# Attention's TensorE order rewritten, with two PSUM banks for the outputs and two for the projections

## The chip, the cores and the metric

The kernel runs on one core of a Trainium2 chip. The time is the device time of one execution in microseconds; the median over several executions is compared. In the profile, PE is TensorE's matmuls, PEld its weight loads, DVE VectorE, ACT ScalarE, POOL GpSimd and SP the engine that issues most transfers.

## The reference

One layer of a hybrid encoder over 1024 positions of width 1024, in float32. The part that matters here is the token mixer:

```python
h = modulate(rms_norm(x, g_pre_mix), sh1, sc1)
bg, cg, u, q, k, v, ga, gb = split(h @ w_in)
y_conv = (bg * causal_dwconv3(cg * u)) @ w_proj_conv
# stick-breaking attention, 8 heads of 64, strictly causal
a[t, s] = sigmoid(z_ts) * prod_{s < j < t} (1 - sigmoid(z_tj)),  z = q k^T / 8
y_attn = (a @ v) @ w_proj_attn
out = (sigmoid(ga) * y_conv + sigmoid(gb) * y_attn) @ w_out
```

A squared-ReLU MLP of width 4096 follows, with a norm and a gate of its own.

## The kernel before

A float32 value is held as a sum of two parts of the type float32r, a high and a low one, and a product is three matmuls (high by high, high by low, low by high). Splitting a tile is a copy on ACT (L104, the high part) and a subtraction on DVE (L91, the low part).

The stage in question runs from about 86 to 437 us. It computes attention for 8 heads and, between attention's steps, the projections of h onto queries, keys and the three inputs of the convolution. Attention is cut into 32 units, one for each head and each group g (0 to 3) of 256 query rows; unit number = 4 x head + g. PE's instructions in this stage stand in an order written out by hand, the string `order`: one word (window) for each unit, one letter for each step.

- `f` is one step of `fill`: one eighth of the contraction of half a projection, three matmuls of 128x512 (`project`, L547). Eight such steps fill one bank; 20 projections of two halves give 320 steps, of which 289 stand in the order and 31 run after it. After the eighth, `use` reads the bank: ACT and DVE copy queries (L569, L570) or keys (L588, L589, L590), DVE or ACT the convolution's inputs (L600, L609, L628).
- `n` is one step of `weights` for the next unit: two matmuls into a bank `z` (L678, L681) for up to 512 keys. ACT then forms two sigmoids (L684 into `pt`, L685 into `a`); when a block of 128 rows is complete, POOL masks its diagonal (L687), DVE runs the product scan over the row (L691) and multiplies (L695). The result is `a`.
- `w` is one step of `attend`: in turns a `turn` (three or four 128x128 transposes of `a` into a bank `tr`, L721, which are then split into `tu` by L104 and L91) and a `weigh` (four matmuls of `tu` with the values into the bank `o`, L732). A weigh stands one turn behind its own transposes, so the last weigh of a unit is the second `w` of the next unit's window. After it `finish` reads the bank with ACT (L741) and DVE (L742, `ot`), and stores. The next unit's first weigh is two `w` steps further on.

The other engines' orders in this stage are made by the framework's scheduler from this program; only PE's is by hand. Of the eight PSUM banks `psm` (tag `mm`) has three, and the pool `pat` has `z` two, `tr` two, `o` one. With one `o` bank a unit's first weigh waits for L742 of the unit before. Writing T(u,k) and W(u,k) for the turn and the weigh number k of unit u, the text below can name steps: unit 9's window `nnffwnffnwffwfwf` holds T(9,0), the last weigh of unit 8, T(9,1) and W(9,0).

After the order is used up, `conv_branch` runs the remaining `fill` steps, with DVE and ACT in an order of the program's.

Of the kernel before, what the change touches and what calls it, by code (L numbers as in the profile page):

```python
# [13 lines left out]
PSUM = bass.MemoryType.PSUM  # L14
# [16 lines left out]
def block_kernel(  # L31
# [28 lines left out]
    def nm(s):  # L60
        uid[0] += 1
        return f"{s}_{uid[0]}"

    def open_pool(es, name, **kw):
        kw = {"bufs": 1, "reuse_waits": "tile", **kw}
        return es.enter_context(tc.tile_pool(name=name, **kw))
# [14 lines left out]
    def bank(pool, tag, bufs=None):  # L81
        return pool.tile([P, HALF], F32, tag=tag, name=nm(tag), bufs=bufs)
# [19 lines left out]
    def split(src, hi, lo, eng=nc.vector):  # L102

        nc.scalar.copy(hi, src)  # L104
        sub(lo, src, f(hi), eng)

    def load_cols(w, m):

        raw = raw_tile((P, KC, P))
        nc.sync.dma_start(raw, w[:, m * P : (m + 1) * P].rearrange("(a p) n -> p a n", p=P))  # L110
        hi = wp.tile([P, KC, P], F32R, tag="wh", name=nm("wh"), bufs=2)
        lo = wp.tile([P, KC, P], F32R, tag="wl", name=nm("wl"), bufs=2)
        split(raw, hi, lo)
        return hi, lo
# [421 lines left out]
        with tc.manual_schedule(engines={mybir.EngineType.PE, mybir.EngineType.SP}):  # L536
            run(order)
    psm_es = ExitStack()
    psm = open_pool(psm_es, "psm", bufs=3, space=PSUM, side="right")


    def project(ps, w, half):

        s = halves[half]
        for k in range(KC):
            for i, (a, b) in enumerate(((0, 0), (0, 1), (1, 0))):
                nc.tensor.matmul(  # L547
                    ps, w[a][:, k, :], hT[b][:, k, s], start=k == 0 and i == 0,
                    stop=k == KC - 1 and i == 2, skip_group_check=True,
                )  # L550
            yield k

    with ExitStack() as es:
        at = open_pool(es, "at")
        pat = open_pool(es, "pat", space=PSUM)
# [78 lines left out]
        def projections(seq):  # L634
            ahead = load_cols(w_in, seq[0][1])
            for n, (begin, m, j) in enumerate(seq):
                w = ahead
                if n + 1 < len(seq):
                    ahead = load_cols(w_in, seq[n + 1][1])
                use = begin(j)  # L640
                for half in range(2):
                    ps = bank(psm, "mm")
                    for k in project(ps, w, half):
                        if k == KC - 1:
                            use(half, ps)
                        yield
# [9 lines left out]
        for p, (n0, n1) in enumerate(CONV):  # L656
            seq += rest[:n0] + qk[2 * p + 2 : 2 * p + 4] + rest[n0 : n0 + n1]
            rest = rest[n0 + n1 :]
        fill = projections(seq + rest)

        def weights_of(hd, i, out):
# [42 lines left out]
        def attend(hd, g, aa):  # L704

            p, e = hd // 2, hd % 2
            own, other = slice(e * HD, (e + 1) * HD), slice((1 - e) * HD, (2 - e) * HD)
            parts, po = {}, None

            def turn(jp):  # L710
                diag = jp == g
                pa = bank(pat, "tr", 2)
                th, tl = parts[jp] = turned[seen[0] % 2]
                seen[0] += 1
                pa3 = pa.rearrange("p (a b) -> p a b", b=P)
                for j in range(2):
                    for t in range(2):
                        if diag and j > t:
                            continue
                        s = (2 * jp + j) * P  # L720
                        nc.tensor.transpose(pa3[:, 2 * j + t, :], aa[t][:, s : s + P], ident)  # L721
                for b in ((slice(0, 2), slice(3, 4)) if diag else (slice(0, 4),)):
                    to = slice(b.start + 1, b.stop + 1)
                    split(pa3[:, b, :], th[:, to, :], tl[:, to, :])

            def weigh(jp):
                nonlocal po
                po = po if jp else bank(pat, "o", 1)
                for j in range(2):
                    v = vs[:, 2 * jp + j, hd, :, :]  # L730
                    for n, part in enumerate(parts[jp]):
                        nc.tensor.matmul(  # L732
                            po[:, : 2 * P], v,
                            part[:, 0:5:4, :] if j and jp == g else part[:, 2 * j + 1 : 2 * j + 3, :],
                            start=jp == 0 and j == 0 and n == 0,
                            stop=jp == g and j == 1 and n == 1,
                        )

            def finish():
                ot = at.tile([P, 2 * P], F32, tag="ot", name=nm("ot"), bufs=1)  # L740
                nc.scalar.copy(ot[own], po[other, : 2 * P])  # L741
                nc.vector.tensor_tensor(ot[own], po[own, : 2 * P], ot[own], op=ALU.add)  # L742
                nc.sync.dma_start(o_d[p, own, 2 * g * P : (2 * g + 2) * P], ot[own])


            for jp in range(g + 1):
                turn(jp)
                yield
                if due:
                    due.pop()()  # L750
                    yield
                due.append(lambda jp=jp: (weigh(jp), jp == g and finish()))
# [5 lines left out]
        for t in turned:  # L758
# [4 lines left out]


        order = """
            ffffffffffffffffffffffffffffffffnffffffnfffffff
            nnfwf ffnnfwfnffwwnfwf nfnwwwnfffwwwnf fnfffffwfffwfwfwnwwffwfffw
            nfwnw fffnwwnfffnfnwffffw nfnwwnnffwffwww nwwwfwwwwnw
            nnfwwf nnffwnffnwffwfwf nfwwnffwnwnfwwf fffwfwfffwwnfwnwwfwff
            wnwn fnffffffwfwfwfnfnnffffw fwwnnwfffnnwwffw ffnfnfffffwfwfwffwfwffwfwfffw  # L770
            wnnwf ffnfnfwwwnffnwf nfffwfwnnwwfwnfwf nfffwffnfwffwfwwfwfwfw
            fwnwfn fffnffwnfnnwwffffffw wfnfwffnwwnwnfffwfffff nnffwfwfwfwffwfffwwfffw
            wnwn fffnnfwwnffnww fnffwwwnffnfnfwww fnffwfwwfnfwwfwfwwff
            wfffnnwffff fnfnwfnwfwfnfwf nfffwwnwnfwfnfwffwf fffffwwfwffwwffffwfwfffwf
        """
        with tc.manual_schedule(engines={mybir.EngineType.PE}):
            for u, window in enumerate(order.split(), -1):
# [766 lines left out]
```

## Time and profile before

| | |
|---|---|
| median of 3 runs | 1422.18 us (1419.94 to 1425.4) |
| profiled execution, its own time | 1429.52 us |
| its span in the profile | 1427.8 us |
| mean granted TensorE clock | 0.989 |
| PE / PEld / DVE / ACT / POOL busy | 96% / 79% / 74% / 46% / 7% |

The profiled execution's time is its span and 1.7 us around it; it was 7.3 us above the median. A matmul's end in the profile is modelled: a 128x512 matmul is shown with 0.39 us, and the next starts 0.23 us after it. So a row of PE that waited shows a wait counted from the modelled end.

### The profile page before, as it was taken

How to read it: one execution, taken by the hardware profiler on the slowest of the kernel's cores; microseconds unless marked ns; L12 is line 12 of the kernel's file. 1: busy time of each engine (PE TensorE's matmuls, PEld its weight loads, DVE VectorE, ACT ScalarE, POOL GpSimd, SP SyncE). 2: the span in 40 equal slices, each digit the busy share in tenths (PEclk: the TensorE clock that was granted, in tenths of full speed). 3: DMA queues.
4: the chain of work that ended last, by engine and by line, in shares of the span. 5: the costliest groups of instructions: out<-in, count | busy, mean ns of one | idle time of the engine just before them, and what ended most of it. 6: DMA issues, size and time to landing. Idle time of an engine off the chain costs nothing.

```text
span 1427.8 us, 17929 instructions
## 1 busy us (share of the span) xinstructions
PE 1370.1 (96%) x6281; PEld 1121.9 (79%) x6281; DVE 1059.4 (74%) x1664; ACT 652.4 (46%) x1317; POOL 93.8 (7%) x188
## 2 busy tenths in 40 slices
PE   5899899999999999999999899999999999999997
PEld 4788777887888888777878688888888888888886
DVE  6727887887876877727736886666554989898988
ACT  5636656665543544334446643333331554334343
POOL 1002111211200000000001000000000000000001
PEclk9899999999999999999999899999999999999999
DMA  8601111111123766728432254243336643414113
GB/s 298 189 15 34 38 30 45 38 37 51 37 95 111 257 232 226 236 103 325 147 105 91 72 170 140 90 140 132 125 117 230 199 141 110 158 46 155 56 59 118
DMA packets 112753, 178.42 MB, mean 125 GB/s; under 512 B 7900, under 2 KB 67344, under 8 KB 112664
## 3 DMA queue, kind: packets, MB, share of 16 engines
q1 hardware_dynamic: 112664, 177.29, 37.3%
q8 instruction: 49, 0.80, 0.2%
q14 instruction: 40, 0.33, 0.1%
HBM read 135.83 MB, written 41.43 MB: 124 GB/s over the span
## 4 chain that ended last, share of the span: by engine, by line
PE 74%; DVE 13%; issue 4%; DMA 4%; ACT 3%; POOL 1%; SPq 0%; DVEq 0%; POOLq 0%; ACTq 0%
PE s L235 27%; PE s L1397 18%; PE mm L547 10%; PE s L904 3%; PE v L509 3%; DVE pt L691 2%; PE s L122 2%; PE s L121 2%; PE s L123 2%; PE o L732 2%; DVE a L695 2%; PE tr L721 2%; DMA wa<-in_w_ada_dram 1%; DVE y L91 1%; DMA raw<-in_w_in_dram 1%
## 5 line engine op out<-in xcount | busy, mean ns | idle before, releaser
L1397 PE MATMUL s<-y,y 128*128 128x512 f32 x1008 | 238.5, 390 | 0.0
L1397 PEld LDWEIGHTS s<-y,y 128*128 128x128 f32 x1008 | 189.2, 188 | 40.4
L547 PE MATMUL mm<-hTh,wh 128*128 128x512 f32 x320 | 129.1, 403 | 0.0
L547 PE MATMUL mm<-hTh,wl 128*128 128x512 f32 x320 | 125.5, 392 | 0.0
L547 PE MATMUL mm<-hTl,wh 128*128 128x512 f32 x320 | 125.5, 392 | 0.0
L104 ACT CAST y<-g 128x512 fp32r<-128x512 f32 x96 | 53.1, 619 | 116.7 <-PE s L1397 97.6
L691 DVE TENSOR_TENSOR_SCAN pt<-pt,dmask 128x128 f32<-128x128 f32 (+3 forms) x64 | 87.2, 1366 | 8.6 <-ACT pt L684 8.2
L235 PE MATMUL s<-mTh,g 128*128 128x512 f32 x256 | 87.1, 405 | 3.7 <-ACT mTh L104 3.7
L1397 PE MATMUL s<-fr,fr 128*128 128x512 f32 x336 | 85.9, 392 | 0.2
L104 ACT CAST tu<-tr 128x512 fp32r<-128x512 f32 (+2 forms) x112 | 49.1, 439 | 78.2 <-PE tr L721 49.4
L91 DVE TENSOR_TENSOR tu<-tr,tu 128x512 fp32r<-128x512 f32 (+2 forms) x112 | 55.1, 493 | 34.5 <-ACT tu L104 33.4
L235 PE MATMUL s<-mTh,h 128*128 128x512 f32 x240 | 79.6, 398 | 0.0
L1397 PEld LDWEIGHTS s<-fr,fr 128*128 128x128 f32 x336 | 62.9, 188 | 15.1 <-DVE fr L91 1.1
L1407 DVE TENSOR_TENSOR ffacc<-s,ffacc 128x512 f32<-128x512 f32 x96 | 65.0, 684 | 12.1 <-PE s L1397 12.0
L132 POOL TENSOR_TENSOR rstd<-var,mhalf 128x1 f32<-128x1 f32 x32 | 22.4, 698 | 766.6 <-DVE var L129 766.5
L235 PE MATMUL s<-y,g 128*128 128x512 f32 x288 | 71.7, 391 | 0.0
L235 PE MATMUL s<-y,h 128*128 128x512 f32 x288 | 71.2, 391 | 0.0
L547 PEld LDWEIGHTS mm<-hTh,wl 128*128 128x128 f32 x320 | 60.2, 188 | 13.4
L547 PEld LDWEIGHTS mm<-hTl,wh 128*128 128x128 f32 x320 | 60.5, 189 | 8.9
L547 PEld LDWEIGHTS mm<-hTh,wh 128*128 128x128 f32 x320 | 60.4, 189 | 8.8
L235 PE MATMUL s<-hTh,t 128*128 128x512 f32 x208 | 66.8, 392 | 0.0
L732 PE MATMUL o<-tu,vs 128*128 128x256 f32 x320 | 56.9, 297 | 9.6 <-DVE ot L742 5.0
(292 smaller groups left out, 3124.6 us busy)
## 6 DMA issues: line engine op xcount, KB each, us to landing
raw<-in_w_in_dram SPq DMA_DIRECT2D x38, 512.0 KB, 4.1
raw<-in_w_mlp_in_dram SPq DMA_DIRECT2D x32, 512.0 KB, 3.9
wa<-in_w_ada_dram SPq DMA_DIRECT2D x24, 512.0 KB, 4.4
f_d<-wl SPq DMA_DIRECT2D x16, 512.0 KB, 5.0
f_d<-wh SPq DMA_DIRECT2D x16, 512.0 KB, 4.8
g<-in_w_mlp_out_dram SPq DMA_DIRECT2D x32, 256.0 KB, 3.5
g<-f_d SPq DMA_DIRECT2D x32, 256.0 KB, 4.0
h<-in_w_mlp_out_dram SPq DMA_DIRECT2D x32, 256.0 KB, 3.3
```

Of the source, the lines that this page charges most:

```text
L91: eng.tensor_tensor(o, a, b, op=ALU.subtract)
L104: nc.scalar.copy(hi, src)
L121: nc.tensor.matmul(ps, lh, rh, start=i == 0, stop=False)
L122: nc.tensor.matmul(ps, lh, rl, start=False, stop=False)
L235: nc.tensor.matmul(ps, l, r, start=first and k == 0 and j == 0, stop=k == nk - 1 and j == 2, skip_group_check=True,)
L509: nc.tensor.matmul(vb[b], l, r, start=k == 0 and i == 0, stop=k == KC - 1 and i == 2, skip_group_check=True,)
L547: nc.tensor.matmul(ps, w[a][:, k, :], hT[b][:, k, s], start=k == 0 and i == 0, stop=k == KC - 1 and i == 2, skip_group_check=True,)
L691: nc.vector.tensor_tensor_scan(pt[:, 0:w][:, ::-1], pt[:, 0:w][:, ::-1], dmask[:, T - w : T][:, ::-1], 1.0, ALU.mult, ALU.max,)
L732: nc.tensor.matmul(po[:, : 2 * P], v, part[:, 0:5:4, :] if j and jp == g else part[:, 2 * j + 1 : 2 * j + 3, :], start=jp == 0 and j == 0 ...
L904: nc.tensor.matmul(ps, l[:, k, s], r, start=k == 0 and i == 0, stop=k == 3 and i == 2, skip_group_check=True,)
L1397: nc.tensor.matmul(ps, l[:, s], r, start=start and j == 0 and n == 0, stop=stop and j == len(fs) - 1 and n == 2, skip_group_check=True,)
L1407: nc.vector.tensor_tensor(o, ps, o, op=ALU.add)
```

## The change

Three edits in one:

- `o` gets two banks in turn in place of one.
- `psm` has two banks in place of three. The first projection (queries of the first two heads) uses the two `o` banks, which are not needed until the second window.
- The order is written anew. Each window holds the same `n` and `w` steps as before, and the total of `f` steps is the same (289); their places, and the number of `f` steps in most windows, differ by one to three.

```diff
-    psm = open_pool(psm_es, "psm", bufs=3, space=PSUM, side="right")
+    psm = open_pool(psm_es, "psm", bufs=2, space=PSUM, side="right")
...
-                    ps = bank(psm, "mm")
+                    ps = bank(pat, "o", 2) if n == 0 else bank(psm, "mm")
...
-                po = po if jp else bank(pat, "o", 1)
+                po = po if jp else bank(pat, "o", 2)
...
-            ffffffffffffffffffffffffffffffffnffffffnfffffff
-            nnfwf ffnnfwfnffwwnfwf nfnwwwnfffwwwnf fnfffffwfffwfwfwnwwffwfffw
-            nfwnw fffnwwnfffnfnwffffw nfnwwnnffwffwww nwwwfwwwwnw
-            nnfwwf nnffwnffnwffwfwf nfwwnffwnwnfwwf fffwfwfffwwnfwnwwfwff
-            wnwn fnffffffwfwfwfnfnnffffw fwwnnwfffnnwwffw ffnfnfffffwfwfwffwfwffwfwfffw
-            wnnwf ffnfnfwwwnffnwf nfffwfwnnwwfwnfwf nfffwffnfwffwfwwfwfwfw
-            fwnwfn fffnffwnfnnwwffffffw wfnfwffnwwnwnfffwfffff nnffwfwfwfwffwfffwwfffw
-            wnwn fffnnfwwnffnww fnffwwwnffnfnfwww fnffwfwwfnfwwfwfwwff
-            wfffnnwffff fnfnwfnwfwfnfwf nfffwwnwnfwfnfwffwf fffffwwfwffwwffffwfwfffwf
+            ffffffffffffffffffffffffffffffffnffffffnfffffff nnfffw fnnfwfnfffwwnwf fnfnfwwfwnfwwfnfw
+            ffnfffffwffwffwfwnwwfwffw wnfnw ffnfwnwfffnfnwfffw nfnwwnnffwfffwww
+            nwwwwwwnww nwnwff nnffwnwfnffffwfw nffwnfwnfwwfnwwf
+            ffffwfwfwwnfwnwwwfff wnwn fnffffffwfwnfffnwnfffw ffffwwfnnwffnnwwffw
+            fnfnfffffwfwfwffwfwfwfwffffw nwnfw ffnfnwwwnffnfw nfffwwnnfwwffwnfwf
+            nfffffwfnfwwfwffwffwwfw nwnw fffnffwnfffwnnwffffffw fwnwnfwwnwnfffwffff
+            nnffwfwfwfwfffwfffwwffw wnfnw ffnnfwwnffnwfw fnffwwwnffnfwnfwfwf
+            fnffwfwwfnwwfwffwfw wnfnfwfffff fnfnwffnnwffwwf nfffwwnnwwffnfwffwf
+            fffffwfwwffwwfffwfwfffwf
```

The first window (47 letters) belongs to unit 0's `n` steps and is unchanged; the windows of units 0 to 31 follow.

## The prediction

> **What bounds the kernel now.** I read the page's head first, then the windows by stage, then PE's timeline through attention for the rows that waited.
>
> ```profile
> span 1427.8 us, 17929 instructions
> PE 1370.1 (96%) x6281; PEld 1121.9 (79%) x6281; DVE 1059.4 (74%) x1664; ACT 652.4 (46%) x1317; POOL 93.8 (7%) x188
> ```
> ```profile
> core 0: us, PE busy (x) PEld busy (x) DVE busy (x) ACT busy (x) POOL busy (x), PEclk, DMA share, GB/s
> 120.00:418.00 298.00, 282.44 (x1527) 236.89 (x1526) 241.96 (x337) 173.85 (x388) 60.91 (x129) 0.99 0.14 40
> 418.00:437.00 19.00, 19.00 (x85) 15.70 (x84) 15.68 (x22) 4.27 (x6) 0.00 (x0) 1.00 0.41 135
> ```
>
> PE is the bound nearly everywhere. In the 298 us in which the order is at work it is idle for 15.6 us by the modelled ends; DVE is busy for 242 of them, 81%, so there is room on DVE on average, though not everywhere. Every instruction that PE issues here stays, so the time can only come out of PE's waits (or go into new ones). These are all the rows of PE that waited, 19 of them:
>
> ```profile
> 134.86 0.74 PE L732 MATMUL o<-tu,vs 128*128 128x256 f32 x4 [0.22 <-DVE ot L742]
> 136.46 0.62 PE L732 MATMUL o<-tu,vs 128*128 128x256 f32 x3 [0.41 <-DVE tu L91]
> 168.95 0.55 PE L721 MATMUL tr<-ident,a 128*128 128x128 f32 x3 [0.42 <-DVE a L695]
> 174.69 0.73 PE L732 MATMUL o<-tu,vs 128*128 128x256 f32 x4 [0.42 <-DVE ot L742]
> 178.74 1.01 PE L732 MATMUL o<-tu,vs 128*128 128x256 f32 x3 [2.87 <-DVE tu L91]
> 186.90 0.62 PE L732 MATMUL o<-tu,vs 128*128 128x256 f32 x3 [0.25 <-DVE tu L91]
> 193.51 0.55 PE L721 MATMUL tr<-ident,a 128*128 128x128 f32 x3 [0.78 <-DVE a L695]
> 200.60 0.74 PE L732 MATMUL o<-tu,vs 128*128 128x256 f32 x4 [1.56 <-DVE ot L742]
> 209.15 0.62 PE L732 MATMUL o<-tu,vs 128*128 128x256 f32 x3 [0.34 <-DVE tu L91]
> 212.98 0.52 PE L721 MATMUL tr<-ident,a 128*128 128x128 f32 x3 [0.35 <-DVE a L695]
> 240.43 0.55 PE L721 MATMUL tr<-ident,a 128*128 128x128 f32 x3 [2.02 <-DVE a L695]
> 275.19 0.74 PE L732 MATMUL o<-tu,vs 128*128 128x256 f32 x4 [0.15 <-DVE ot L742]
> 285.99 0.62 PE L732 MATMUL o<-tu,vs 128*128 128x256 f32 x3 [0.71 <-DVE tu L91]
> 315.16 0.55 PE L721 MATMUL tr<-ident,a 128*128 128x128 f32 x3 [0.47 <-DVE a L695]
> 335.08 0.74 PE L732 MATMUL o<-tu,vs 128*128 128x256 f32 x4 [1.88 <-DVE ot L742]
> 348.75 0.55 PE L721 MATMUL tr<-ident,a 128*128 128x128 f32 x3 [0.50 <-DVE a L695]
> 355.55 0.55 PE L721 MATMUL tr<-ident,a 128*128 128x128 f32 x3 [0.26 <-DVE a L695]
> 365.35 0.55 PE L721 MATMUL tr<-ident,a 128*128 128x128 f32 x3 [0.66 <-DVE a L695]
> 388.10 0.74 PE L732 MATMUL o<-tu,vs 128*128 128x256 f32 x4 [0.80 <-DVE ot L742]
> ```
>
> They sum to 15.1 us in three kinds: six weighs that wait for the one `o` bank (L742, 5.0), five that wait for their own split (L91, 4.6), eight turns that wait for `a` (L695, 5.5). The price of a step, and what a row understates, from a quiet stretch:
>
> ```profile
> 398.77 0.64 PE L732 MATMUL o<-tu,vs 128*128 128x256 f32 x4
> 399.25 0.40 PE L547 MATMUL mm<-hTh,wh 128*128 128x512 f32 x1
> 399.48 0.40 PE L547 MATMUL mm<-hTl,wh 128*128 128x512 f32 x1
> 399.94 0.40 PE L547 MATMUL mm<-hTh,wh 128*128 128x512 f32 x1
> ```
>
> A weigh costs 0.48 (398.77 to 399.25), an `f` step 0.69 (399.25 to 399.94). One matmul follows the other after 0.23 but is shown 0.40 long, so each wait costs 0.17 more than its bracket: 15.1 + 19 x 0.17 = 18.3 us. That is the most that this change can take out as waits.
>
> **The change part by part.** *The second output bank* removes the wait for L742 at all six: 5.0 + 6 x 0.17 = 6.0 us. What is late next at each? Two places matter:
>
> ```profile
> 175.67 2.28 DVE L691 TENSOR_TENSOR_SCAN pt<-pt,dmask 128x1024 f32<-128x1024 f32 x1
> 177.99 0.69 DVE L91 TENSOR_TENSOR tu<-tr,tu 128x512 fp32r<-128x512 f32 x1
> ```
> ```profile
> 332.80 0.40 PE L547 MATMUL mm<-hTh,wl 128*128 128x512 f32 x1
> 333.28 0.69 DVE L91 TENSOR_TENSOR tu<-tr,tu 128x512 fp32r<-128x512 f32 x1
> ```
>
> At 174.69 PE would come 0.59 earlier (0.42 + 0.17), but three microseconds on it stands until DVE has run a 2.28 scan and the L91 behind it (177.99); DVE sets that time, so the 0.59 comes back in the next wait. At 335.08 PE could start at 332.80 + 0.23 = 333.03, but its own split ends at 333.28 + 0.69 = 333.97: 0.94 of the 2.05 stays. For the other four I hand back 0.3 (134.86, where the new word has one `f` less between T(2,0) and W(2,0)). Net 6.0 - 0.6 - 0.9 - 0.3 = 4.2 us.
>
> *The turns that wait for `a`.* I count the PE work between a unit's last `n` and its first turn in the old and the new words. It moves by: unit 6 (row 168.95) one `f` less; 9 (193.51) a short turn less, 0.25; 11 (212.98) the same; 14 (240.43) two `f` more; 22 (315.16) 0.2 more; 25 (348.75) 0.2 less; 26 (355.55) one `f` more; 27 (365.35) an `f` and a little more, 0.9. With the time at which `a` is ready left as it is, the eight losses (bracket + 0.17) go from 0.6, 0.95, 0.5, 2.2, 0.65, 0.65, 0.45, 0.8 to 1.3, 1.2, 0.5, 0.8, 0.45, 0.85, 0, 0: 6.8 to 5.1, a gain of 1.7.
>
> *The weighs that wait for their split.* Unit 18 (285.99) has one `f` more between T(18,1) and its weigh, a gain of 0.7; 2 and 10 (136.46, 209.15) cancel at 0.45 each; unit 6 (178.74) has one `f` more, but comes earlier by the 0.59 above and stays; 186.90 stays. Gain 0.7.
>
> *New places.* Units 7 and 8, 16, 17 and 29 lose cover without waiting now: window 7 has no `f` left between its turns (`nwwwwwwnww`), T(17,0) has an `f` less ahead of it, W(16,0) one and a half, W(29,1) two and a bit, less what PE gains at 388. Their slack stands in no row quoted here; each is bounded by nothing and by about an `f`, so 0 to 2.8 together. The rows that wait by a turn's cover (0.4 to 0.9) are nearest, so I charge 0.5 for each of the four, 2.0.
>
> *Two projection banks.* A half may start only when the half two before it is evacuated, in place of three before. The tightest places:
>
> ```profile
> 113.54 0.69 DVE L590 TENSOR_TENSOR kl<-mm,ks 64x512 fp32r<-64x512 f32 x1 [0.49 <-ACT ks L589]
> 330.95 0.69 DVE L590 TENSOR_TENSOR kl<-mm,ks 64x512 fp32r<-64x512 f32 x1 [1.24 <-ACT ks L589]
> ```
> ```profile
> 114.28 0.39 PE L547 MATMUL mm<-hTh,wh 128*128 128x512 f32 x1
> 331.20 0.40 PE L547 MATMUL mm<-hTh,wh 128*128 128x512 f32 x1
> ```
>
> The first pair touches (evacuated at 114.23, next use of that bank under two at 114.28), the second overlaps by 0.44; the new words put half an `f` more into the second. The other halves stand farther apart. I charge 0.4; the ends are 0 and, if the other engines' order slips by half an `f` at each of the sixteen halves of queries and keys, 16 x 0.35 = 5.6. The first projection in the two `o` banks meets no weigh: unit 0's first weigh comes in window 1. Whether those banks come free later than the ones used now is open; all banks of the stage before are read by
>
> ```profile
> 85.34 2.73 DVE L91 TENSOR_TENSOR vs<-v,vs 128x512 fp32r<-128x512 f32 x4 [7.68 <-ACT vs L104]
> ```
>
> 88.07, and PE starts here at 86.6, so 0 to 1.5; I take nothing, since no start of the present banks is late. DMAs: the order moves weight loads by a window at most, in a stage where the engines are busy at a 0.14 share; nothing.
>
> Sum: 4.2 + 1.7 + 0.7 - 2.0 - 0.4 = 4.2 us less. The profiled span goes from 1427.8 to 1423.6, and its time from 1429.5 to 1425.3; in the median's terms, 1422.2 x (1 - 4.2/1427.8) = 1418.0, 0.3% faster. A measurement of this kernel tells about 0.5%, 7.1 us, from no change.
>
> **The clock.** One wait has a consequence of its own:
>
> ```profile
> 178.00:185.00 7.00, 6.26 (x25) 5.74 (x26) 4.87 (x9) 2.14 (x6) 0.50 (x3) 0.52 0.04 9
> ...
> 330.00:340.00 10.00, 8.12 (x46) 6.65 (x45) 5.37 (x10) 3.91 (x10) 1.25 (x4) 1.00 0.27 85
> ```
>
> After the 2.87 us at 178.74 the granted clock is 0.52 for 7 us; around the 1.88 us at 335.08 it is 1.00. At half clock PE does 3.4 us less work there. Little of it is to be won: in that stretch turns and weighs stand back to back, and at full clock each would wait for its split instead. I take 0 in the sum, with 3.4 as the far end. The Trainium skill (TensorE: Matmul & The Clock Gate, HAM oscillation) puts the limit at idle gaps above about 3.4 us; by that a gap of 2.87 would have cost no clock and nothing could be won by shortening it. The trace disagrees with it here, by its 0.52.
>
> **The rivals.** *The waits only move to DVE.* For it: where PE waits longest DVE is full (the scan and L91 above stand back to back), and PE that comes earlier meets the same DVE queue. Against it: 81% busy over the stage, and one of the three largest waits (335.08) stood beside 5.4 of 10 us of DVE (the 330 row above). It gives the gain of that row alone, 1.1, less the bank's 0.4: 1421.5.
>
> *Two projection banks stop PE.* The slower one: ACT and DVE take evacuations in the scheduler's order, among splits and scans; with a bank less, a late L590 or L570 stops not only the projection but, since PE runs in order, every step behind it, and DVE's next scan with it. For it: the two pairs above, without margin. It decides once the evacuations come an `f` step (0.69) later against PE than now at sixteen halves: 16 x 0.69 = 11, less the 4.6 of the other terms, 6.4 slower, 1428.6; at 0.73 or more the result is past 0.5% slower, 1429.3. Against it: only two of the halves are near now. The Trainium skill (Perfetto Trace Analysis, Matmuls) asks that matmul groups rotate through PSUM banks so that an evacuation overlaps the next group; it speaks for the outputs' second bank and against the projections' lost one, and the rows above price both.
>
> *The cover works better than at fixed ready times.* If the scheduler moves DVE's order with PE's, splits that PE needs come forward, and the new words fit what they were counted against badly here. Then the 2.0 of new places is not paid, two thirds of the 18.3 go, and the clock's dip with them: about 12, 1410.
>
> **How the numbers follow.** Forecast 0.37; only moved 0.18; projection banks 0.17; better cover 0.28. The range reaches from below the better cover to the projection banks' case: 1407 to 1429, with about 0.06 below and 0.12 above. Over 0.5% faster (under 1415.1): the better cover's 0.28 and a fifth of the forecast's, 0.35. Slower by over 0.5%: most of the third, 0.13, and 0.05 for unforeseen orders of DVE, 0.18. The rest, 0.47, is between.
>
> **What would show it.** Right: no PE row waits for L742; rows that wait for L695 at 240 and 355 to 365 shrink or go; the one at 168.95 grows to about 1.1; the attention stretch is some 4 us shorter and everything behind it keeps its length. Wrong: PE rows on `mm` (L547) that wait for L590, L570 or L609 (the banks); new waits for L91 of the size of those that went (only moved); a stage behind attention that changes its length, which nothing above provides for.

## The result and the profile after

| | before | after |
|---|---|---|
| median of 6 runs | 1423.91 us (1419.94 to 1426.16) | 1413.3 us (1411.81 to 1415.06) |
| ratio | | 0.992, interval 0.9907 to 0.9933 |
| profiled execution, its own time / span | 1429.52 / 1427.8 us | 1413.2 / 1411.3 us |

The change takes 0.8% off, 11.4 us by the ratio (10.6 between the medians); 4.2 us were predicted. The head of the page, after:

```profile
span 1411.3 us, 17955 instructions
PE 1363.5 (97%) x6281; PEld 1120.2 (79%) x6281; DVE 1058.4 (75%) x1664; ACT 651.3 (46%) x1317; POOL 103.9 (7%) x188
```

The windows by stage come next: up to the first L547, from there to the first matmul of the convolution's product (L904), and the rest. First before, then after; the columns are length, busy time and instruction count of each engine, clock, DMA share, GB/s.

```profile
0.00:86.56 86.56, 67.37 (x289) 54.47 (x290) 54.51 (x110) 48.11 (x97) 10.67 (x25) 0.94 0.61 201
86.56:436.87 350.31, 334.75 (x1761) 280.24 (x1760) 270.16 (x376) 193.31 (x422) 62.32 (x134) 0.99 0.15 44
436.87:1427.80 990.93, 967.95 (x4233) 787.22 (x4231) 734.70 (x1179) 410.96 (x800) 20.86 (x29) 0.99 0.44 147
```
```profile
0.00:84.13 84.13, 63.83 (x289) 51.45 (x290) 54.52 (x110) 48.14 (x97) 10.67 (x25) 0.94 0.63 207
84.13:421.21 337.08, 330.56 (x1761) 279.99 (x1760) 268.81 (x376) 192.96 (x422) 72.34 (x134) 0.99 0.15 46
421.21:1411.30 990.09, 969.07 (x4233) 788.74 (x4231) 735.04 (x1179) 410.19 (x800) 20.86 (x29) 0.99 0.43 147
```

Of the 16.5 us between the two spans, 13.2 lie in the stage that was changed (350.31 to 337.08) and 0.8 behind it. The 2.4 ahead of it are not the change's: nothing there was edited, and the two executions differ there in when the clock is halved (38.0 to 48.2 us before, 39.0 to 42.4 after, at 0.50 and 0.51). In the changed stage PE does the same 1761 records of work, and its idle time falls from 15.6 (350.31 - 334.75) to 6.5 us. PE's timeline, after; these are all its rows in the stage that waited:

```profile
164.99 0.55 PE L721 MATMUL tr<-ident,a 128*128 128x128 f32 x3 [0.43 <-DVE a L695]
174.77 0.62 PE L732 MATMUL o<-tu,vs 128*128 128x256 f32 x3 [2.89 <-DVE tu L91]
182.79 0.44 PE L721 MATMUL tr<-ident,a 128*128 128x128 f32 x2 [0.55 <-DVE a L695]
196.45 0.55 PE L721 MATMUL tr<-ident,a 128*128 128x128 f32 x3 [0.21 <-DVE a L695]
212.36 0.61 PE L732 MATMUL o<-tu,vs 128*128 128x256 f32 x3 [0.24 <-DVE tu L91]
232.80 0.52 PE L721 MATMUL tr<-ident,a 128*128 128x128 f32 x3 [0.53 <-DVE a L695]
320.64 0.47 PE L547 MATMUL mm<-hTh,wh 128*128 128x512 f32 x1 [0.56 <-DVE kl L590]
334.86 0.55 PE L721 MATMUL tr<-ident,a 128*128 128x128 f32 x3 [0.40 <-DVE a L695]
```

Eight rows in place of 19, 5.8 us in place of 15.1. With 0.17 for each row, as the prediction counts, 7.2 us in place of 18.3: the waits account for 11.1 of the 13.2. No row waits for L742 any more; five turns wait for `a` (units 6, 8, 10, 14 and 25, by the order of the L695 rows that release them), two weighs for their split, one `f` step for a projection's bank.

### The profile page after: what moved, and what is told of

Read it like the earlier page. It is cut to its first block, busy times and chain, and to the rows that moved or that the text cites. A ratio compares the mean times of both kernels' runs of the same rounds, so it can differ in the third digit from the quotient of the medians.

```text
span 1411.3 us, 17955 instructions
## 1 busy us (share of the span) xinstructions
PE 1363.5 (97%) x6281; PEld 1120.2 (79%) x6281; DVE 1058.4 (75%) x1664; ACT 651.3 (46%) x1317; POOL 103.9 (7%) x188
## 4 chain that ended last, share of the span: by engine, by line
PE 82%; DVE 9%; DMA 3%; issue 3%; ACT 2%; POOL 1%; SPq 0%; DVEq 0%; POOLq 0%; ACTq 0%
PE s L235 29%; PE s L1397 20%; PE mm L547 12%; PE s L904 3%; PE s L122 3%; PE s L121 3%; PE s L123 3%; PE v L509 2%; PE o L732 2%; PE tr L721 2%; DVE pt L691 2%; DMA raw<-in_w_in_dram 1%; DVE a L695 1%; PE z L678 1%; PE z L681 1%
## 5 line engine op out<-in xcount | busy, mean ns | idle before, releaser
L547 PE MATMUL mm<-hTh,wh 128*128 128x512 f32 x304 | 122.5, 403 | 0.6 <-DVE kl L590 0.6
L547 PE MATMUL mm<-hTh,wl 128*128 128x512 f32 x304 | 119.0, 392 | 0.0
L547 PE MATMUL mm<-hTl,wh 128*128 128x512 f32 x304 | 119.0, 391 | 0.0
L1407 DVE TENSOR_TENSOR ffacc<-s,ffacc 128x512 f32<-128x512 f32 x96 | 64.9, 685 | 11.1 <-PE s L1397 11.1
L687 POOL TENSOR_SCALAR_AFFINE_SELECT a<-a 128x128 f32<-128x128 f32 x64 | 61.4, 960 | 138.0 <-ACT a L685 120.7
L547 PEld LDWEIGHTS mm<-hTh,wl 128*128 128x128 f32 x304 | 57.1, 188 | 12.7
L91 DVE TENSOR_TENSOR y<-g,y 128x512 fp32r<-128x512 f32 x96 | 62.0, 685 | 4.4 <-PE s L1397 3.0
L547 PEld LDWEIGHTS mm<-hTh,wh 128*128 128x128 f32 x304 | 57.2, 188 | 9.4 <-PE tr L721 0.8
```

The lines of the kernel that those rows point to most:

```text
L91: eng.tensor_tensor(o, a, b, op=ALU.subtract)
L547: nc.tensor.matmul(ps, w[a][:, k, :], hT[b][:, k, s], start=k == 0 and i == 0, stop=k == KC - 1 and i == 2, skip_group_check=True,)
L687: nc.gpsimd.affine_select(a[:, i * P : w], a[:, i * P : w], pattern=[[-1, P]], compare_op=ALU.is_gt, fill=0.0, base=0, channel_multiplier=1,)
L1407: nc.vector.tensor_tensor(o, ps, o, op=ALU.add)
```

## Experiments

The first three take the change apart: banks without the order, order without the banks, and the projections' lost bank by itself.

**Both bank edits, the old order.**

```diff
-psm bufs=3      +psm bufs=2
-ps = bank(psm, "mm")       +ps = bank(pat, "o", 2) if n == 0 else bank(psm, "mm")
-bank(pat, "o", 1)          +bank(pat, "o", 2)
```

> The banks of the changed kernel (outputs two, projections two, first projection in the output banks) with the order of before. Theory A (the second output bank carries the gain, the new order only fits it): most of the 10.6 us between the medians comes, 7 us or more, ratio 0.995 or less, and no PE row waits for L742. Theory B (the new order carries it, the bank is a condition): the six waits for L742, 6.0 us, go, but part comes back at the splits behind them and a projection's bank costs something: 2 to 4 us, ratio 0.997 to 0.999, with the eight waits for a (L695) still 4 us or more.

Measured: 0.9992 (0.9979 to 1.0005). All six waits for L742 are gone, and other rows of PE's timeline have come or grown:

```profile
134.18 0.62 PE L732 MATMUL o<-tu,vs 128*128 128x256 f32 x3 [0.85 <-DVE tu L91]
...
176.42 1.01 PE L732 MATMUL o<-tu,vs 128*128 128x256 f32 x3 [3.44 <-DVE tu L91]
...
199.99 0.55 PE L721 MATMUL tr<-ident,a 128*128 128x128 f32 x3 [1.01 <-DVE a L695]
...
276.19 0.55 PE L721 MATMUL tr<-ident,a 128*128 128x128 f32 x3 [0.52 <-DVE a L695]
```

The second row is the return that the prediction named (2.87 to 3.44, the 0.57 that PE came earlier). The third and fourth stand behind weighs that waited for L742 before (200.60, 275.19): PE passes the weigh and stops at the next turn, the fourth time for longer than the 0.15 that went there. The brackets fall from 15.1 to 13.4 only, and the waits for `a` grow to 7.4. This is theory B, with even less left of the gain: 1.1 us by the ratio where it said 2 to 4.

**The new order, the old banks.** The diff's new order alone.

> The order of the changed kernel with the banks of before (outputs one, projections three). In the changed kernel's trace eleven first weighs start before the L742 of the unit before has ended, 7.4 us in sum, so with one bank they would wait that long. Theory A: the new order without the bank is no better than the kernel before, ratio 0.999 to 1.003. Theory B: the 10.6 us gain less 7.4 for the waits, plus up to 0.7 for the projection's bank: 3 to 4 us faster, ratio 0.997 to 0.998; PE rows that wait for L742 sum to 5 to 8 us, those for L695 stay near 2.

Measured: 0.995 (0.993 to 0.997). The waits of PE, grouped by what they wait for (us in total, times, longest):

```profile
PE o L732 <- DVE ot L742: 4.6, 8, 1.4
PE o L732 <- DVE tu L91: 3.3, 3, 2.9
PE tr L721 <- DVE a L695: 1.7, 5, 0.6
```

Beside before's 5.0, 4.6 and 5.5, the order by itself leaves the waits for L742 nearly as they were and takes 3.8 us from the turns. With 7.1 us by the ratio it is worth more than either theory said.

**Two projection banks, nothing else.** `psm` from three banks to two.

> Only the projections' banks are cut, three to two; the output bank stays one, the order that of before. Prices the lost bank by itself. The prediction's term: 0.4 us, ratio 1.000 to 1.001, one PE row on mm waiting 0.3 to 0.6 us for L590. Its rival (projection banks stop PE at many halves): several us, ratio 1.003 or more, and many rows on mm that wait for L570, L590 or L609.

Measured: 0.9997 (0.9985 to 1.001). Two new rows, on PE's timeline:

```profile
84.23 0.50 PE L547 MATMUL mm<-hTh,wh 128*128 128x512 f32 x1 [1.40 <-DVE vs L91]
...
329.79 0.47 PE L547 MATMUL mm<-hTh,wh 128*128 128x512 f32 x1 [0.41 <-DVE kl L590]
```

The later one is the second of the prediction's two pairs (overlap 0.44). The other pair does not wait. The first is the stage's first `f` step: it waits for a bank that the stage before still reads (`vs`). No such row stands in the changed kernel or in the run with both bank edits, where the first projection uses the `o` banks. So, by these profiles, that edit saves 1.40 us which the cut from three banks to two would cost by itself, and the prediction's 0.4 holds only together with it.

The next four ask why the order gains more than counted. Is cover counted in `f` steps exact? Does DVE's order make the difference?

**Two `f` more ahead of the turn that waited 2.02** (T(14,0)), taken from a later window, in the old order.

```diff
-fwwnnwfffnnwwffw ffnfnfffffwfwfwffwfwffwfwfffw
+fffwwnnwfffnnwwffw ffnfnfffffwfwfwffwfwffwfwfw
```

> The kernel before, with one edit in its order: two f steps stand in front of T(14,0), taken from the end of the window after. Tests the prediction's counting rule (a turn's wait shrinks by the PE work put ahead of it, with the time at which a is ready as it is): the 2.02 us for L695 near 240 us becomes 0.65, all other waits as before, the stage 1.4 us shorter. If the other engines' order answers to such an edit, the wait differs from 0.65 by more than 0.3, or waits change at places that the edit doesn't touch.

One execution: 1427.78. Executions of the kernel before lay between 1422.3 and 1430.5 beside it, so a single one is read by its rows:

```profile
241.24 0.55 PE L721 MATMUL tr<-ident,a 128*128 128x128 f32 x3 [0.65 <-DVE a L695]
...
267.05 0.39 PE L732 MATMUL o<-tu,vs 128*128 128x256 f32 x1 [0.40 <-DVE tu L91]
```

2.02 less two `f` (1.38) is 0.64: to the hundredth, cover behind the last `n` counts in full. But a new wait of 0.40 appears where the count of `f` had shifted, 26 us on, and the 0.15 for L742 near 275 us is gone: waits also change where the edit doesn't reach.

**DVE's reads of banks queued behind its multiplies,** with both bank edits and the old order: L742 and the projections' reads (L570, L590, L609, L628) may not stand ahead of the last multiply (L695) that the program has issued. DVE instructions between a scan and its multiply fall from 51 to 36 in the traces.

```diff
+        def behind(emit):
+            if not product:
+                return emit()
+            with tc.issue_after(product[-1]):
+                return emit()
```

> The old order with the new banks (as in the first experiment), and DVE's order changed by hand in one respect: L742 and the reads of the projections' banks (L570, L590, L609, L628) are queued behind the last multiply (L695) that the program has emitted, so that they don't stand between a product scan and its multiply; fourteen of the 51 DVE instructions that stand there go behind. PE's order is that of before. Theory 'DVE's order decides when a is ready': the waits for L695, 7.4 us in the first experiment, fall to 5 or less and the time by 2 to 4 us against it, ratio to the kernel before 0.996 to 0.998. Theory 'DVE's amount of work decides': the waits move among themselves, sum within 1 us, ratio 0.998 to 1.000. Late evacuations would show as PE rows on mm.

Measured: 1.0007 (0.9993 to 1.0021), and PE waits as long as before (15.2 in brackets). Beside the run with the banks alone, one wait of 0.79 went, an `n` step waits for the first time (0.54), and these grew, from 1.01 and 0.20:

```profile
198.94 0.55 PE L728 MATMUL tr<-ident,a 128*128 128x128 f32 x3 [1.44 <-DVE a L702]
...
207.57 0.61 PE L739 MATMUL o<-tu,vs 128*128 128x256 f32 x3 [1.61 <-DVE tu L91]
```

(Lines are 7 higher in this kernel: L728 is the turn, L739 the weigh, L702 the multiply.) What DVE does earlier for one, it does later for another.

**The same rule on the changed kernel.**

> The changed kernel with the same rule on DVE (L742 and the projections' reads behind the last multiply). Only 2.1 us of PE's waits are for L695 there, in five rows, so 'DVE's order' can give 1 us at most (ratio to before 0.991), and late reads of the two projection banks can cost: with PE rows on mm of 1 us or more the ratio is 0.993 or above.

Measured: 0.9916 (0.9898 to 0.9935), 1415.28 us: the changed kernel's own ratio. So this rule for DVE's order brings nothing on the old order and adds nothing to the new one. Other orders of DVE were not tried.

**Three `f` more ahead of the 2.89 wait,** in the changed kernel, taken from a window nine units on.

```diff
-nfnwwnnffwfffwww        +nfnwwnnffwfffwwfffw
-...fwfwfwfwffffw        +...fwfwfwfwfw
```

> The changed kernel with three f steps more in front of the weigh that waits 2.89 us near 175 us (window 6), taken from the end of window 15. If DVE sets the time there, PE work put into the wait is free: the wait falls by 2.06 to about 0.8, the window that gives the steps up loses nothing, and the stage is 2 us shorter, ratio to before 0.9905; the half-clock stretch behind it may go as well. If the steps only push the wait on (the eighth step of a half falls among them, and its reads, 2.9 us of DVE, with it), the wait or the next one stays and the time is that of the changed kernel, 0.992.

Measured: 0.9943 (0.9923 to 0.9963), 1418.41 us: 0.2% slower than the changed kernel by the two ratios, whose intervals overlap. On PE's timeline:

```profile
176.57 0.61 PE L732 MATMUL o<-tu,vs 128*128 128x256 f32 x3 [0.79 <-DVE tu L91]
...
180.39 0.53 PE L732 MATMUL o<-tu,vs 128*128 128x256 f32 x1 [1.67 <-DVE tu L91]
...
250.94 0.47 PE L547 MATMUL mm<-hTh,wh 128*128 128x512 f32 x1 [1.24 <-DVE kl L590]
```

The wait itself falls by the three `f` (2.89 - 2.07 = 0.82), but the next weigh waits 1.67 and a projection 1.24; farther on a turn (211.02) waits 1.22 and a weigh (265.05) 1.40. Three `f` moved also move the end of every half in nine windows, and with it the reads that DVE has to place.

The last three ask from where cover counts. A unit's two blocks of rows end their keys at different `n` steps; the multiply of the second block releases the turn that waits. L says that cover counts from the last `n`, as the prediction did; F says from the `n` that completes the first block, because DVE goes through two scans and two multiplies in a row.

**Unit 14: two `f` between the first block's `n` and the last.**

```diff
-wnwn fnffffffwfwfwfnfnnffffw ... ffwfwfffw
+wnwn fnffffffwfwfwfnfffnnffffw ... ffwfwfw
```

> The kernel before, two f steps put between unit 14's first block of rows (its n steps) and its second, taken from the end of window 15 as in the fourth experiment. The work between the last n and T(14,0) stays 3.9 us, that between the first block's last n and T(14,0) grows from 5.2 to 6.6. Theory L (the prediction's count, from the last n): the wait near 240 us stays 2.0. Theory F (DVE works through both blocks of the unit, two scans and two multiplies, 5.0 us, so the count starts at the first block's n): it falls by 1.4 to about 0.65, as it did with the two steps behind the last n.

First the kernel before (PE's first block's `n`, and DVE), then this one:

```profile
232.62 0.28 PE L678 MATMUL z<-ks,qs 128*128 128x256 f32 x1
...
234.26 1.48 DVE L691 TENSOR_TENSOR_SCAN pt<-pt,dmask 128x640 f32<-128x640 f32 x1
...
236.50 0.83 DVE L695 TENSOR_TENSOR a<-a,pt 128x640 f32<-128x640 f32 x1
...
237.56 1.75 DVE L691 TENSOR_TENSOR_SCAN pt<-pt,dmask 128x768 f32<-128x768 f32 x1
239.42 0.96 DVE L695 TENSOR_TENSOR a<-a,pt 128x768 f32<-128x768 f32 x1
```
```profile
229.18 0.28 PE L678 MATMUL z<-ks,qs 128*128 128x256 f32 x1
...
233.28 0.81 DVE L695 TENSOR_TENSOR a<-a,pt 128x640 f32<-128x640 f32 x1
...
234.01 1.75 DVE L691 TENSOR_TENSOR_SCAN pt<-pt,dmask 128x768 f32<-128x768 f32 x1
...
235.88 0.96 DVE L695 TENSOR_TENSOR a<-a,pt 128x768 f32<-128x768 f32 x1
...
236.90 0.55 PE L721 MATMUL tr<-ident,a 128*128 128x128 f32 x3 [0.56 <-DVE a L695]
```

From the first block's `n` to the end of the second multiply it is 7.76 us before (232.62 to 240.38) and 7.66 here (229.18 to 236.84), though the last `n` stands two `f` later. So the two `f` count in full, and the wait is 0.56 in place of 2.02: F. The execution took 1423.1 beside 1425.45, but single executions scatter by more than that.

**Unit 14: one `f` moved from between the `n` steps to behind them.** `...fnfnnffffw` becomes `...fnnnfffffw`.

> The kernel before, the one f step between unit 14's first and second block moved behind its last n. Work from the last n to T(14,0) grows by 0.69, from the first block's n it stays. Theory L: the wait near 240 us falls from 2.0 to 1.3. Theory F: it stays 2.0, within 0.2.

```profile
237.28 0.52 PE L721 MATMUL tr<-ident,a 128*128 128x128 f32 x3 [1.76 <-DVE a L695]
```

It lies nearer to F's 2.0 than to L's 1.3, a little outside F's band. The rest is PE's own: its `n` steps now follow one another, and the third starts 0.46 after the matmul ahead of it (229.84 to 230.30) where 0.23 is usual (233.76 to 233.99 before). PE thus comes 0.23 later, and F's wait is 1.79.

**Unit 22: two `f` moved from behind the last `n` to ahead of it.** `fffnffwnfnnwwffffffw` becomes `fffnffwnfffnnwwffffw`.

> The kernel before, in unit 22's n steps (window 21) two f steps moved from behind the last n to between the first and the second block. Work from the last n to T(22,0) falls by 1.4, from the first block's n it stays. Theory L: the wait near 315 us grows from 0.47 to 1.9. Theory F: it stays at 0.5, within 0.3.

```profile
313.64 0.55 PE L721 MATMUL tr<-ident,a 128*128 128x128 f32 x3 [0.47 <-DVE a L695]
```

By L two `f` of cover are lost and the wait is 1.9; it is 0.47, what it was before (315.16). Work between the two blocks counts in full in a second unit, and from the other side.

Put together, with each kernel's loss as its brackets and 0.17 a row:

| kernel | rows | loss, us | less than 18.3 | less by the ratio, us |
|---|---|---|---|---|
| banks, old order | 17 | 16.3 | 2.0 | 1.1 |
| two projection banks | 21 | 19.9 | -1.6 | 0.4 |
| reads behind, old order | 19 | 18.4 | -0.1 | -1.0 |
| order, old banks | 16 | 12.3 | 6.0 | 7.1 |
| changed, three `f` moved | 13 | 11.3 | 7.0 | 8.1 |
| changed, reads behind | 11 | 8.6 | 9.7 | 12.0 |
| changed | 8 | 7.2 | 11.1 | 11.4 |

The ratio's column is (1 - ratio) x 1425; its intervals are 2 to 3 us to each side, and the rows' column lies inside all of them but one: for two projection banks it is 0.2 outside. What separates these kernels is thus the waits of PE, and the question is how to count them ahead.

## Why the prediction was right in direction and short in size

The measured time lies in the range, but in the case to which the prediction gave 0.35 (over 0.5% faster), not in the likeliest. Of its signs, no row waits for L742, the waits at 240 and 355 to 365 shrank or went, and the stages behind kept their length. The row at 168.95, which was to grow to about 1.1, is 0.43. Losses by kind, by the prediction's own count:

| | before | predicted | after |
|---|---|---|---|
| weighs that wait for L742 | 6.0 | 0 | 0 |
| weighs that wait for their split, in the old places | 5.5 | 6.6 (5.5 - 0.7 + 1.8 handed back) | 3.1 |
| turns: the eight that waited | 6.8 | 5.1 | 1.9 |
| turns and weighs in new places | 0 | 2.0 | 1.5 |
| projections | 0 | 0.4 | 0.7 |
| sum | 18.3 | 14.1 | 7.2 |

**The step that failed: the turns.** The words were counted from the last `n`, with the time at which `a` is ready left as it was. It did not stay: from the last `n` to the end of the second multiply it is 6.54 us before and 5.03 after the change at unit 22, 5.75 and 4.05 at unit 9. Units 14 and 22 show that work put between a unit's two blocks of rows counts in full; the prediction took it for nothing, and the new words put `f` steps there at 11, 14 and 22. Counted from the first block's `n`, the change in cover at units 6, 9, 11, 14, 22, 25, 26 and 27 is -0.2, 0, +1.15, +2.97, +2.04, 0, +0.68 and +1.36 us, and the eight losses come to 2.4 (0.8, 0.95 and 0.65 at units 6, 9 and 25), against 1.9 measured and 5.1 predicted.

The better count is not exact either, and its sum comes near because two misses cancel. At unit 14 it leaves no loss, and 0.70 stands there (232.80, 0.53 and 0.17); the prediction's own count gave 0.8. The timelines of PE and DVE say why, first the kernel before, then the changed one:

```profile
231.49 1.23 DVE L91 TENSOR_TENSOR wl<-raw,wh 128x1024 fp32r<-128x1024 f32 x1 [0.26 <-ACT wh L104]
```
```profile
223.34 0.28 PE L678 MATMUL z<-ks,qs 128*128 128x256 f32 x1
...
223.93 1.22 DVE L91 TENSOR_TENSOR wl<-raw,wh 128x1024 fp32r<-128x1024 f32 x1 [0.26 <-ACT wh L104]
...
226.36 1.49 DVE L691 TENSOR_TENSOR_SCAN pt<-pt,dmask 128x640 f32<-128x640 f32 x1
...
231.69 0.96 DVE L695 TENSOR_TENSOR a<-a,pt 128x768 f32<-128x768 f32 x1
```

The first scan starts 3.02 after its `n`, where it was 1.64 before (232.62 to 234.26): in neither kernel is it this `n` that DVE waits for. DVE works almost without a pause (none over 0.15) from a split of weights, for which it last waited, to the end of the second multiply. That takes 8.89 us before, 8.72 after and 8.79 in the run with two `f` between the blocks; from the first block's `n` it is 7.76, 9.31 and 7.66. So at unit 14 the count starts with the work that is queued on DVE ahead of both blocks. At other units it starts at the last `n` after all, because DVE stands idle for it before the second scan: at unit 26 in the kernel before, at unit 8 in the changed one.

```profile
352.56 1.76 DVE L691 TENSOR_TENSOR_SCAN pt<-pt,dmask 128x768 f32<-128x768 f32 x1 [0.82 <-ACT pt L684]
```
```profile
181.39 0.69 DVE L691 TENSOR_TENSOR_SCAN pt<-pt,dmask 128x256 f32<-128x256 f32 x1 [0.29 <-ACT pt L684]
```

Cover thus counts from where DVE last waited. This is read from the traces; no run moved work ahead of both blocks to test it.

At unit 9 the count leaves 0.95 and nothing is left. Two things fill it. PE loses 0.72 (182.79, 0.55 and 0.17) at T(8,0), which the new words put between unit 9's `n` steps. And `a` is ready 5.42 after the first block's `n` in place of 6.10: DVE's read L609 (0.69) stood between the second scan and its multiply before and follows the multiply now, so DVE's order does matter here. The two, 0.72 and 0.68, are more than the 0.95. With one output bank and the new order the two are 0.33 and 0.11, which leaves 0.51; the row there is 0.34 and 0.17.

Of the new places one of the four came, unit 8's 0.55; units 16, 17 and 29 have no row. Unit 10's turn (0.21) was not foreseen, nor unit 11's weigh (212.36, 0.24), whose new word has no `f` left between T(11,3) and it. 2.0 was charged where 1.5 came.

**The second output bank.** All six waits went, as predicted. With the new words 1.8 of the 6.0 was to come back; on the old order 3.3 of the 5.0 in brackets did, 0.4 of it at a projection's bank and more at turns that the prediction did not look at (199.99 and 276.19). The return at 178.74 was right (0.57 for 0.59), and so was its reason: after the change the same weigh still waits 2.89, and DVE sets it, with a scan and the split back to back:

```profile
171.71 2.28 DVE L691 TENSOR_TENSOR_SCAN pt<-pt,dmask 128x1024 f32<-128x1024 f32 x1
174.03 0.69 DVE L91 TENSOR_TENSOR tu<-tr,tu 128x512 fp32r<-128x512 f32 x1
```

The 0.94 charged at 335.08 did not come there, neither on the old order nor on the new. With the new order the bank edits are worth 5.1 us by the rows (12.3 to 7.2), some 4 by the ratios (0.995 to 0.992, whose intervals overlap a little): eight weighs wait for L742 where there is one bank, and the turns behind them have cover.

**Weighs and their splits.** 6.6 was predicted, 3.1 came, in one row: this term was missed by as much as the turns. Part of it is the prediction's sum. At unit 6 the 0.59 was charged twice, once as handed back by the bank and once against the `f` more: 3.04 + 0.59 - 0.69 is 2.94, and 3.06 came. The 0.94 at 335.08 and the 0.4 for the projection's bank are one delay counted twice. With the banks alone PE loses 0.60 at the projection's bank (328.68, 0.43 and 0.17) and 0.3 inside the weigh behind it:

```profile
330.59 0.95 PE L732 MATMUL o<-tu,vs 128*128 128x256 f32 x4
```

Such a weigh is 0.64 to 0.65 long where nothing holds it. With the new order PE loses 0.73 at the projection's bank and nothing at the weigh. Unit 18's wait went, as predicted; those of units 2, 7 and 10, 1.5 in all, went where the prediction cancelled or kept them. The order alone does it too (3.3 in three rows). No run separates the reasons there; that the split, like the turn, was ready earlier than a fixed time is argued, not shown.

**The projections' banks.** 0.4 was predicted; 0.41 came at the place that was named on the old order, 0.56 on the new. The rival in which the banks stop PE fell. At the stage's start the prediction left 0 to 1.5 open for the `o` banks and took nothing, and no `f` step of the first projection waits for an output bank. The 1.40 there came only without them; the ratio of that run, 0.9997, is too coarse to tell it.

**The rivals.** *Waits only move to DVE* describes the reordered DVE (1.0007) and most of the banks on the old order (0.9992), not the change. *Better cover* (1410) was nearest: the new places were paid in part (1.5 of 2.0), and 11.1 of the 18.3 went where it said two thirds. Its mechanism was half right: at unit 9 DVE's order did change in PE's favour, and splits that come forward would fit the weighs, which no run shows. At the turns it was mostly the start of the count.

**The clock.** 0 was taken in the sum. After the 2.89 wait the clock is halved for 3.41 us, where it was for 6.83 before:

```profile
175.60:179.00 3.40, 3.27 (x16) 3.07 (x15) 2.53 (x7) 2.01 (x6) 0.62 (x3) 0.50 0.00 0
```

But runs with the old order show 3.41 as well and the new order with one output bank shows 6.83, so the difference, at most 1.7 us of the 13.2 in the stage, is not the change's.

## What to carry to other kernels

When a step waits for a chain on another engine, do not count its cover from the last input by habit. Look in the trace for the place where that engine last stood idle, and count from what it waited for there: all that is queued behind it, other work too, is one run (8.7 to 8.9 us at unit 14 in three kernels). A second buffer removed its own wait here and handed most of it to the next one, unless the order behind it had cover: the banks alone gave 0.9992, the order alone 0.995, both 0.992. Moving a filler step also moves where every later group of fillers ends and is read, so a local gain of 2 us was lost over nine windows.

## What the runs showed of the hardware

The clock can halve after waits of PE much shorter than three microseconds, and does not do so each time. Here are the windows from 1.43 us after the start of the same turn, which waited 2.02 us (unit 14), first in the run with two projection banks (the turn at 237.27), then in the kernel before (240.43):

```profile
238.70:242.10 3.40, 3.40 (x12) 2.88 (x11) 2.01 (x4) 3.33 (x8) 0.00 (x0) 0.50 0.08 19
```
```profile
241.86:245.26 3.40, 3.40 (x18) 2.45 (x16) 2.01 (x4) 3.33 (x8) 0.00 (x0) 1.00 0.08 19
```

At a clock of 0.50 PE gets through 12 records where it gets through 18 at 1.00. The Trainium skill (TensorE: Matmul & The Clock Gate, HAM oscillation) warns of idle gaps above about 3.4 us; here gaps of 2.87 and 2.02 were followed by a halved clock, and in the kernel with three `f` moved so were gaps of 1.67 and 1.40 (180.39 and 265.05; 0.50 from 180.6 to 183.8 and from 265.8 to 269.0). What decides whether a gap of 2 us is followed by one was not tried.
